# A block of matmul and elementwise groups appended behind a Fourier and Hyena encoder layer

## The chip, the cores and the metric

One NeuronCore of a Trainium2 chip runs the kernel. The metric is the device time of one execution in microseconds. The core's engines work side by side, each with a queue of its own that runs in order: TensorE (PE: matmuls; PEld: its weight loads), VectorE (DVE), ScalarE (ACT), GpSimd (POOL) and SyncE (SP), which here issues nearly all the DMAs. SBUF is the working memory of 128 partitions, PSUM the eight banks that matmuls write to, each with 512 float32 columns per partition.

## The reference

One layer of an encoder over 2048 positions of 1024 channels:

```python
for i in range(DEPTH):                      # DEPTH = 1
    h = rmsnorm(x, g_mix[i])
    p = jnp.einsum('bld,de->ble', h, w_in[i])
    u_f = p[..., :FOURIER_WIDTH]
    u_h = p[..., FOURIER_WIDTH:]
    y_f = rmsnorm(fourier_mix(u_f), g_fourier[i])
    y_h = rmsnorm(hyena_mix(u_h, ...), g_hyena[i])
    y = jnp.concatenate([y_f, y_h], axis=-1)
    x = x + jnp.einsum('ble,ed->bld', y, w_out[i])
    hm = rmsnorm(x, g_mlp[i])
    a = jnp.square(jax.nn.relu(jnp.einsum('bld,df->blf', hm, w_fc1[i])))
    x = x + jnp.einsum('blf,fd->bld', a, w_fc2[i])
return rmsnorm(x, g_final)
```

`fourier_mix` is a two-dimensional FFT over positions and the 64 channels of a group, of which the real part is kept; `hyena_mix` is a short convolution, then two long convolutions done as FFTs, each multiplied by a gate. Nothing of the appended block enters the result.

## The kernel before

The kernel goes through its stages in order of the program: the projection by `w_in` (lines 329 to 447), the Fourier group and the Hyena filters (459 to 687), the Hyena convolutions (688 on), the output projection (912 on), the first MLP matrix (`fc1`, 1127 on) and the second (`fc2`, 1244 on). The DFTs are matmuls with small tables. The large products are made of three matmuls each: an operand is split by `split` (line 181) into a high part in the type float32r (`FR`), written by ACT at line 184, and a low part, the difference, written by VectorE or POOL at line 185. `mm3` (line 196) then multiplies high by high, high by low and low by high in the lines 198, 199 and 200. These float32r matmuls of 128 rows, 128 weight columns and 512 moving columns are the greater part of the TensorE instructions. The profile writes float32r as f32 in a matmul's row and as fp32r in a cast's.

Some smaller matmuls are in plain float32. The prediction uses four of them. L465 has 512 moving columns and stands in a loop of 16. L729 has 256 columns. L736 has 128, taken from `G[:, :, 4q+j]`, where `G` holds 64 x 32 x 2 floats per partition, so that it reads pairs of neighbours, one pair every 64 floats. L765 has 64 weight columns: `gate` calls it twice, first with the output in the partitions 0 to 63 and then in 64 to 127 of one bank,

```python
h = slice(64 * sp, 64 * sp + 64)
nc.tensor.matmul(p[h], lhsT=b1[:, h], rhs=rows, start=True, stop=True)
```

A framework sets semaphores between the engines by the tiles that they share, and a scheduler with priorities sets the order in each queue. Tiles come from pools; `pa` gives a PSUM bank, `load` (line 171) a tile with its DMA on SP (line 173). `wfd` is a scratch tensor in DRAM, written and read early, in the projection.

The end of the program is `fc2` for the second half of the positions. SP has fetched the last weights by 2213 us. The last tile is added up by VectorE (L1322), squared and normalised by ACT, VectorE and POOL (L1292 to L1306), and stored from SP and ACT (L1307). The profile's "PEclk" is the clock that the throttle granted to TensorE, as a share of full speed.

## Time and profile before

| | us |
|---|---|
| two runs | 2299.6 and 2293.75 |
| median of the two | 2296.68 |
| span of the profiled execution | 2296.7 |

The page does not say which run was profiled; the table sets its span beside the median of the runs. The page gives for each engine the busy time, its share of the span and the number of instructions, for each queue of DMAs its packets and megabytes, and the chain of work that ended last with the shares of the engines and lines in it. Rows of groups give line, engine, operation, tile written and tiles read, shapes and count, then busy time in us and mean ns of one, then the idle time ahead of them with what ended it. Rows of the timeline give the start in us, the length of the merged stretch in us, and the same names; since the end of a matmul is modelled and matmuls overlap, what a matmul costs is read from the distance between starts. Rows of DMA issues end with the KB of each and the median us from issue to landing. Rows of windows give the stretch, its length, the busy time and count of PE, PEld, DVE, ACT and POOL, the granted clock, the DMA share and GB/s.

### The profile page before, as it was taken

The numbers are of one execution on the slowest core, as the hardware profiler recorded it, in microseconds if no ns is written. First come the engines' busy times: TensorE is split into PE (matmuls) and PEld (weight loads), VectorE is DVE, ScalarE is ACT, GpSimd is POOL, SyncE is SP. The second block draws the span as 40 slices with busy tenths as digits, with TensorE's granted clock in tenths as the row PEclk, the third lists the DMA queues.
The fourth block names the chain that finished last, engine by engine and source line by source line (L and its number), as shares of the span: only waits on it lengthen the run. The fifth ranks groups of instructions, "written<-read, shape, count | busy, mean of one in ns | idle before, by whom it ended". The sixth has DMA issues, their size and how long they took to land.

```text
span 2296.7 us, 31041 instructions
## 1 busy us (share of the span) xinstructions
PE 2238.5 (97%) x11025; PEld 1855.9 (81%) x11025; DVE 1501.3 (65%) x2254; ACT 1108.8 (48%) x1849; POOL 826.0 (36%) x627
## 2 busy tenths in 40 slices
PE   8999999999999989998999989999999999999998
PEld 6887788799788858886888878888888888888886
DVE  6999676777578774458444465444477666866667
ACT  6555211566366564455555565555543333533333
POOL 3444323576476611146555546555400000000000
PEclk9999999999999999999999999999999999999999
DMA  8535886689987766667444475444489766866631
GB/s 270 184 133 198 315 304 247 223 289 324 337 264 210 214 194 188 180 197 234 156 149 150 151 247 164 152 152 151 143 316 344 246 189 196 297 197 194 192 119 74
DMA packets 298798, 487.31 MB, mean 212 GB/s; under 512 B 17478, under 2 KB 141712, under 8 KB 294418
## 3 DMA queue, kind: packets, MB, share of 16 engines
q1 hardware_dynamic: 292977, 470.91, 62.2%
q10 hardware_dynamic: 5664, 14.41, 1.8%
q8 instruction: 87, 1.43, 0.3%
q14 instruction: 70, 0.57, 0.1%
HBM read 314.64 MB, written 169.05 MB: 211 GB/s over the span
## 4 chain that ended last, share of the span: by engine, by line
PE 85%; DVE 5%; DMA 4%; ACT 3%; issue 2%; POOL 1%; SPq 0%; ACTq 0%; DVEq 0%; POOLq 0%
PE p2u L198 5%; PE p2u L199 5%; PE p2u L200 5%; PE p1u L198 5%; PE p1u L200 5%; PE p1u L199 5%; PE pu L200 4%; PE pu L199 4%; PE pu L198 4%; PE p2v L198 3%; PE p2v L199 3%; PE p2v L200 3%; PE pk L610 2%; PE p1v L198 2%; PE p1v L200 2%; PE pz L729 2%
## 5 line engine op out<-in xcount | busy, mean ns | idle before, releaser
L184 ACT CAST qahm<-ra 128x1024 fp32r<-128x1024 f32 x110 | 115.9, 1053 | 345.2 <-PE p2u L199 172.0
L185 DVE TENSOR_TENSOR qalm<-ra,qahm 128x1024 fp32r<-128x1024 f32 x110 | 134.7, 1225 | 153.7 <-ACT qahm L184 151.8
L1293 POOL TENSOR_TENSOR acc<-acc,gfin 128x512 f32<-128x512 f32 x4 | 5.1, 1278 | 631.9 <-DMA out<-acc 624.7
L198 PE MATMUL pu<-wh,xh 128*128 128x512 f32 x512 | 204.3, 400 | 5.6 <-ACT wh L187 4.4
L199 PE MATMUL pu<-wl,xh 128*128 128x512 f32 x512 | 201.7, 394 | 3.7 <-DVE wl L188 3.6
L200 PE MATMUL pu<-wh,xl 128*128 128x512 f32 x512 | 201.6, 394 | 1.2 <-DVE xl L185 1.2
L199 PE MATMUL p2u<-qblm,qahm 128*128 128x512 f32 x504 | 196.3, 390 | 0.0
L198 PE MATMUL p2u<-qbhm,qahm 128*128 128x512 f32 x504 | 196.1, 390 | 0.0
L200 PE MATMUL p2u<-qbhm,qalm 128*128 128x512 f32 x504 | 196.0, 390 | 0.0
L185 DVE TENSOR_TENSOR qblm<-rb,qbhm 128x1024 fp32r<-128x1024 f32 x110 | 134.1, 1219 | 2.6 <-ACT qbhm L184 2.4
L393 POOL TENSOR_TENSOR acc<-acc,cw 128x512 f32<-128x512 f32 x45 | 59.9, 1332 | 196.8 <-DVE acc L370 193.5
L184 ACT CAST ahm<-s 128x512 fp32r<-128x512 f32 x124 | 76.7, 621 | 100.9 <-PE p1v L199 55.3
L185 POOL TENSOR_TENSOR alm<-W,ahm 128x512 fp32r<-128x512 f32 x63 | 86.2, 1369 | 97.8 <-ACT ahm L184 97.8
L198 PEld LDWEIGHTS pu<-wh,xh 128*128 128x128 f32 x512 | 97.2, 190 | 26.3 <-ACT wh L187 4.8
L199 PEld LDWEIGHTS pu<-wl,xh 128*128 128x128 f32 x512 | 97.3, 190 | 25.3 <-DVE wl L188 4.9
L184 ACT CAST qbhm<-rb 128x1024 fp32r<-128x1024 f32 x110 | 115.3, 1048 | 4.7 <-DMA rb<-in_w_fc 3.4
L200 PEld LDWEIGHTS pu<-wh,xl 128*128 128x128 f32 x512 | 97.2, 190 | 22.8 <-DVE xl L185 2.8
L198 PEld LDWEIGHTS p2u<-qbhm,qahm 128*128 128x128 f32 x504 | 94.7, 188 | 20.0 <-issue 0.3
L200 PEld LDWEIGHTS p2u<-qbhm,qalm 128*128 128x128 f32 x504 | 94.7, 188 | 19.6
L199 PEld LDWEIGHTS p2u<-qblm,qahm 128*128 128x128 f32 x504 | 94.7, 188 | 19.5
L198 PE MATMUL p1u<-bm,ahm 128*128 128x512 f32 x252 | 100.3, 398 | 9.4 <-ACT ku L1155 9.4
L184 ACT CAST ahm<-W 128x512 fp32r<-128x512 f32 x94 | 57.5, 615 | 101.5 <-PE p1u L199 101.5
(397 smaller groups left out, 6428.6 us busy)
## 6 DMA issues: line engine op xcount, KB each, us to landing
W<-in_w_fc SPq DMA_DIRECT2D x66, 512.0 KB, 4.6
spec<-ks SPq DMA_DIRECT2D x32, 1024.0 KB, 6.2
ks<-spec SPq DMA_DIRECT2D x64, 512.0 KB, 4.9
rb<-td SPq DMA_DIRECT2D x64, 512.0 KB, 4.1
ra<-a1m SPq DMA_DIRECT2D x56, 512.0 KB, 3.9
ra<-a0m SPq DMA_DIRECT2D x54, 512.0 KB, 5.8
rb<-in_w_fc SPq DMA_DIRECT2D x46, 512.0 KB, 4.9
f<-in_w_fc SPq DMA_DIRECT2D x16, 1024.0 KB, 8.2
```

The lines of the kernel that those rows point to most:

```text
L184: nc.scalar.copy(hi, src)
L185: (eng or nc.vector).tensor_sub(lo, src, hi)
L198: nc.tensor.matmul(o, lhsT=lh, rhs=rh, start=start, stop=False, skip_group_check=more)
L199: nc.tensor.matmul(o, lhsT=lh, rhs=rl, start=False, stop=False, skip_group_check=more)
L200: nc.tensor.matmul(o, lhsT=ll, rhs=rh, start=False, stop=stop, skip_group_check=more)
L393: nc.gpsimd.tensor_add(m1, m1, cw[:, 3, :])
L610: nc.tensor.matmul(p[:, 128 * j : 128 * j + 128], lhsT=f2[:, 4 * q + j, :], rhs=self.G[:, :, 4 * q + j], start=True, stop=True)
L729: nc.tensor.matmul(p[:, 256 * sp : 256 * sp + 256], lhsT=e1[:, sp, :], rhs=zz[:, :, lo : lo + 16], start=True, stop=True)
L1293: nc.gpsimd.tensor_mul(acc[i][:, c], acc[i][:, c], gfin[:, c])
```

## The change

Behind `fc2` a block is added in a pool of its own. It loads 2 MB (`src`, 16 KB in each partition), splits half of it into a high and a low part (`phi`, `plo`), casts a quarter to bf16 (`half`), and then issues groups of matmuls, each in one form. The forms are float32r with 512, 256 and 128 columns, with moving operands in steps of 8 and of 64 bytes, in two blocks and with an offset; bf16; float32 with 128 and 512 columns; float32 and float32r with 64 of the 128 rows, by turns of the halves; float32 with 64 rows and 64 weight columns, by turns of the four corners; float32 with 64 weight columns; and a mixture. After these come three of each of some elementwise operations on VectorE, ACT and POOL, and five stores of 256 KB to `wfd`. The lines that the diff adds begin at 1477.

```diff
@@ -1474,6 +1474,91 @@
             run(fc2(mp, blk, gfin, {} if blk else begun))
 
 
+    with pool("probe") as pp:
+        src = load(pp, "src", [P, 8, 512], A["f2"].rearrange("p (a f) c -> p a (f c)", a=8))
+        hi, lo = (pp.tile([P, 4, 512], FR, tag=n, name=n) for n in ("phi", "plo"))
+        split(hi, lo, src[:, 0:4])
+        half = pp.tile([P, 2, 512], BF16, tag="half", name="half")
+        nc.scalar.copy(half, src[:, 0:2])
+        out1 = pp.tile([P, 2, 512], F32, tag="po1", name="po1")
+        out2 = pp.tile([P, 2, 512], F32, tag="po2", name="po2")
+        b0, b1, b2 = pa("probe0"), pa("probe1"), pa("probe2")
+        w = hi[:, 0, 0:128]
+        wide = hi.rearrange("p a c -> p (a c)")
+
+        for k in range(16):
+            nc.tensor.matmul(b0, lhsT=w, rhs=hi[:, k % 4, :], start=True, stop=True)
+        for k in range(16):
+            nc.tensor.matmul(b0[:, 0:256], lhsT=w, rhs=hi[:, k % 4, 0:256], start=True, stop=True)
+        for k in range(16):
+            nc.tensor.matmul(b0[:, 0:128], lhsT=w, rhs=hi[:, k % 4, 0:128], start=True, stop=True)
+        for k in range(16):
+            nc.tensor.matmul(b0, lhsT=w, rhs=wide[:, 1024 * (k % 2) : 1024 * (k % 2) + 1024 : 2], start=True, stop=True)
+        for k in range(16):
+            nc.tensor.matmul(b0, lhsT=w, rhs=hi[:, k % 4, :].rearrange("p (a b) -> p b a", b=16), start=True, stop=True)
+        for k in range(16):
+            nc.tensor.matmul(b0, lhsT=w, rhs=hi[:, 0:2, 0:256], start=True, stop=True)
+        for k in range(16):
+            nc.tensor.matmul(b0, lhsT=w, rhs=wide[:, 8 : 520], start=True, stop=True)
+        for k in range(16):
+            nc.tensor.matmul(b0, lhsT=half[:, 0, 0:128], rhs=half[:, k % 2, :], start=True, stop=True)
+        for k in range(12):
+            nc.tensor.matmul(b0[:, 0:128], lhsT=src[:, 5, 0:128], rhs=src[:, k % 4, 0:128], start=True, stop=True)
+        for k in range(12):
+            nc.tensor.matmul(b0, lhsT=src[:, 5, 0:128], rhs=src[:, k % 4, :], start=True, stop=True)
+        for k in range(12):
+            h = slice(64 * (k % 2), 64 * (k % 2) + 64)
+            nc.tensor.matmul((b0, b1)[k % 2][:, 0:256], lhsT=src[h, 5, 0:128], rhs=src[h, k % 4, 0:256], start=True, stop=True)
+        for k in range(12):
+            h = slice(64 * (k % 2), 64 * (k % 2) + 64)
+            nc.tensor.matmul((b0, b1)[k % 2], lhsT=hi[h, 2, 0:128], rhs=hi[h, k % 4, :], start=True, stop=True)
+        for k in range(24):
+            h = slice(64 * (k % 2), 64 * (k % 2) + 64)
+            o = slice(64 * ((k % 2) ^ (k // 2 % 2)), 64 * ((k % 2) ^ (k // 2 % 2)) + 64)
+            nc.tensor.matmul((b0, b1)[k // 2 % 2][o, 0:128], lhsT=src[h, 5, 0:64], rhs=src[h, k % 4, 0:128], start=True, stop=True)
+        for k in range(16):
+            h = slice(64 * (k % 2), 64 * (k % 2) + 64)
+            o = slice(64 * ((k % 2) ^ (k // 2 % 2)), 64 * ((k % 2) ^ (k // 2 % 2)) + 64)
+            nc.tensor.matmul((b0, b1)[k // 2 % 2][o], lhsT=src[h, 5, 0:64], rhs=src[h, k % 4, :], start=True, stop=True)
+        for k in range(12):
+            o = slice(64 * (k % 2), 64 * (k % 2) + 64)
+            nc.tensor.matmul(b0[o, 0:128], lhsT=src[:, 5, 0:64], rhs=src[:, k % 4, 0:128], start=True, stop=True)
+        for k in range(8):
+            nc.tensor.matmul(b0, lhsT=w, rhs=hi[:, k % 4, :], start=True, stop=True)
+            for j in range(2):
+                h = slice(64 * j, 64 * j + 64)
+                nc.tensor.matmul(b2[h, 0:128], lhsT=src[h, 5, 0:64], rhs=src[h, j, 0:128], start=True, stop=True)
+        nc.tensor.matmul(b0, lhsT=w, rhs=hi[:, 0, :], start=True, stop=True)
+        nc.tensor.matmul(b1, lhsT=w, rhs=hi[:, 1, :], start=True, stop=True)
+        for k in range(3):
+            nc.vector.tensor_copy(out1[:, 0, :], b0)
+        for k in range(3):
+            nc.vector.tensor_add(out1[:, 1, :], out1[:, 0, :], b1)
+        for k in range(3):
+            nc.vector.tensor_add(out1[:, 1, :], src[:, 0, :], src[:, 1, :])
+        for k in range(3):
+            nc.vector.tensor_copy(out1, src[:, 0:2, :])
+        for k in range(3):
+            nc.vector.tensor_scalar(out=out1, in0=src[:, 0:2, :], scalar1=1.5, scalar2=2.0, op0=ALU.mult, op1=ALU.add)
+        for k in range(3):
+            nc.scalar.copy(out2[:, 0, :], b0)
+        for k in range(3):
+            nc.scalar.copy(out2, src[:, 2:4, :])
+        late = pp.tile([P, 2, 512], F32, tag="po3", name="po3")
+        nc.gpsimd.tensor_copy(late[:, 0, 0:1], out1[:, 0, 0:1])
+        for k in range(3):
+            nc.gpsimd.tensor_add(late[:, 1, :], src[:, 0, :], src[:, 1, :])
+        for k in range(3):
+            nc.gpsimd.tensor_copy(late, src[:, 0:2, :])
+        for k in range(3):
+            nc.gpsimd.tensor_scalar(out=late, in0=src[:, 0:2, :], scalar1=1.5, scalar2=2.0, op0=ALU.mult, op1=ALU.add)
+        nc.sync.dma_start(wfd[0:128, :], out1[:, 0, :])
+        nc.sync.dma_start(wfd[128:256, :], out2[:, 0, :])
+        nc.sync.dma_start(wfd[256:384, :], late[:, 0, :])
+        nc.sync.dma_start(wfd[384:512, :], late[:, 1, :])
+        nc.sync.dma_start(wfd[512:640, :], out1[:, 1, :])
+
+
 # ---- launch: one core; the host only arranges the inputs ----
 def kernel(**inputs):
     import concourse.bacc as bacc
```

No instruction that was there is moved. On POOL the new rows follow the last products with gfin (1293); the scheduler has put the three additions of line 1550, written after the small copy of line 1548, ahead of it (`po` with a number is one of the tiles po1 to po3: 19659 is po1, 19939 is po3, named late in the code):

```order
 L1293 TENSOR_TENSOR acc<-acc,gfin 128x512 [waits Activation_49] x2
-L1515 UNCONDITIONAL_BRANCH
-L1515 ISA [waits barrier_Pool_Activation_PE_DVE_SP_gather]
+L1550 TENSOR_TENSOR po_19939<-src 128x512 [waits DMAHW5_49,DMAHW4_49,DMAHW6_49,DMAHW2_49,DMAHW7_49,DMAHW1_49,DMAHW0_49]
+L1550 TENSOR_TENSOR po_19939<-src 128x512 [waits Pool_49] x2
+L1548 COPY po_19939<-po_19659 128x1 [waits DVE_49]
+L1552 COPY po_19939<-src 128x1024 [waits Pool_49] x3
+L1554 TENSOR_SCALAR po_19939<-src 128x1024 [waits Pool_49] x3
```

The additions wait for DMAs alone; the copy of line 1548 waits for VectorE, and all that follows it on POOL stands behind it. On SP the load and the five stores stand behind the two last stores of the result (po_19660 is po2, which ACT writes):

```order
 L1307 DMA out<-acc 128x512 [waits DMAHW6_49,DVE_49]
 L1307 DMA out<-acc 128x512 [waits DMAHW0_49,DVE_49]
-L1515 UNCONDITIONAL_BRANCH
+L173 DMA src<-in_f 128x4096 [waits DMAHW2_49,Activation_49]
+L1556 DMA wfd<-po_19660 128x512 [waits DMAHW3_49,Activation_49]
+L1555 DMA wfd<-po_19659 128x512 [waits DMAHW4_49,DVE_49]
+L1559 DMA wfd<-po_19659 128x512 [waits DMAHW5_49]
+L1557 DMA wfd<-po_19939 128x512 [waits DMAHW6_49,Pool_49]
+L1558 DMA wfd<-po_19939 128x512 [waits DMAHW7_49]
```

The store of ACT's tile comes first there and the two of POOL's tile last. On VectorE, the operations of the lines 1534 to 1542 stand in the order of the code:

```order
 L1306 TENSOR_SCALAR acc<-acc,nw_s 128x512 [waits DVE_49,Pool_49]
-L1515 UNCONDITIONAL_BRANCH
+L185 TENSOR_TENSOR plo<-src,phi 128x2048 [waits DMAHW2_49,Activation_49]
+L1534 COPY po_19659<-probe_19661 128x512 [waits PE_49]
+L1534 COPY po_19659<-probe_19661 128x512 [waits DVE_49] x2
+L1536 TENSOR_TENSOR po_19659<-po_19659,probe_19662 128x512 [waits DVE_49,PE_49]
+L1536 TENSOR_TENSOR po_19659<-po_19659,probe_19662 128x512 [waits DVE_49] x2
+L1538 TENSOR_TENSOR po_19659<-src 128x512 [waits DVE_49] x3
+L1540 COPY po_19659<-src 128x1024 [waits DVE_49] x3
+L1542 TENSOR_SCALAR po_19659<-src 128x1024 [waits DVE_49] x3
```

The first copy there waits for TensorE, and the operations that read only `src` stand behind it. On TensorE the groups stand in the order of the code behind the last matmul of `fc2`, and the first of them waits for ACT.

## Prediction before the change was run

> **What bounds the kernel now.** I read the page's busy shares first, then the chain that ended last, then the end of the timeline, because the change stands behind the last instruction.
>
> ```profile
> PE 2238.5 (97%) x11025; PEld 1855.9 (81%) x11025; DVE 1501.3 (65%) x2254; ACT 1108.8 (48%) x1849; POOL 826.0 (36%) x627
> PE 85%; DVE 5%; DMA 4%; ACT 3%; issue 2%; POOL 1%; SPq 0%; ACTq 0%; DVEq 0%; POOLq 0%
> ...
> core 0: 2296.7 us, clock 0.991
> ```
>
> TensorE is the bound: 97% busy, 85% of the chain. The end of the timeline:
>
> ```profile
> 2285.00 0.39 PE L200 MATMUL p2u<-qbhm,qalm 128*128 128x512 f32 x1
> ...
> 2287.04 0.39 PE L200 MATMUL p2u<-qbhm,qalm 128*128 128x512 f32 x1
> ...
> 2290.00 2.92 SPq L1307 DMA_DIRECT2D out<-acc  x2
> ...
> 2292.07 0.49 DVE L1306 TENSOR_SCALAR acc<-acc,nw_s 128x512 f32<-128x512 f32 x1
> 2292.81 0.34 ACTq L1307 DMA_DIRECT2D out<-acc  x1
> ```
>
> The reader is to see three things. From 2285.00 to 2287.04 fp32r matmuls of 512 columns start at nine equal steps, so one costs 0.227 us. TensorE then has nothing for the last 9 us. SP issues its last store by 2292.92, and the program ends 3.9 us after the last issue starts (2296.7 less 2292.81). Every added instruction stands last in its queue, and all but the independent POOL adds hang on each other: load, cast, matmuls, VectorE, POOL, stores. So I sum along that chain.
>
> **Load and cast.** SP cannot issue the 2 MB load of src before 2292.92.
>
> ```profile
> td<-f SPq DMA_DIRECT2D x16, 1024.0 KB, 5.5
> out<-acc SPq DMA_DIRECT2D x2, 256.0 KB, 2.6
> 20.00:25.00 5.00, 5.00 (x23) 4.08 (x22) 5.00 (x10) 5.00 (x9) 0.00 (x0) 1.00 1.01 414
> ```
>
> No 2 MB transfer is in the trace. From 256 KB at 2.6 us to 1 MB at 5.5 us the slope is 3.9 us per MB, which gives 9.3 us; the best rate of a window, 414 GB/s, gives 5.1 us behind some 1.6 us of latency, 6.7 us. I take 8.0, since nothing else moves then. The cast to phi has 2048 columns:
>
> ```profile
> L184 ACT CAST qahm<-ra 128x1024 fp32r<-128x1024 f32 x110 | 115.9, 1053 | 345.2 <-PE p2u L199 172.0 <-PE p2v L199 104.6 <-PE p2m L199 44.7
> L184 ACT CAST ahm<-s 128x512 fp32r<-128x512 f32 x124 | 76.7, 621 | 100.9 <-PE p1v L199 55.3 <-PE p1m L199 26.2 <-PE p1u L199 14.2
> ```
>
> 512 more columns cost 0.43 us, so it takes 1.05 + 0.86 = 1.9. With 0.1 us for each handover TensorE starts at 2303.0. The cast to bf16, the plo difference and the first POOL adds run beside the matmuls and cost nothing while these last over 6 us.
>
> **Clock.** TensorE will have been idle 16 us.
>
> ```profile
> 11.12 0.80 PE L198 MATMUL pu<-wh,xh 128*128 128x512 f32 x1 [4.36 <-ACT wh L187]
> ...
> 13.64 0.63 PE L198 MATMUL pu<-wh,xh 128*128 128x512 f32 x1
> 14.06 0.63 PE L199 MATMUL pu<-wl,xh 128*128 128x512 f32 x1
> 14.49 0.47 PE L200 MATMUL pu<-wh,xl 128*128 128x512 f32 x1
> 14.80 0.40 PE L198 MATMUL pu<-wh,xh 128*128 128x512 f32 x1
> 15.03 0.40 PE L199 MATMUL pu<-wl,xh 128*128 128x512 f32 x1
> ```
>
> After an idle stretch at the start, matmuls are 0.43 us apart for 3.5 us, then 0.23. I add half of 3.5 us: 1.75.
>
> **Full-array matmuls.** fp32r at 512 columns costs 0.227. fp32 is dearer; in these rows of the timeline each group is followed by the next without a wait:
>
> ```profile
> 409.29 1.88 PE L465 MATMUL pf<-uf,e1f 128*128 128x512 f32 x4
> 411.00 1.05 PE L542 MATMUL pk<-wo,emb 128*128 128x128 f32 x8
> ...
> 702.07 1.89 PE L729 MATMUL pz<-zz,e1z 128*128 128x256 f32 x8
> 703.79 1.06 PE L736 MATMUL pz<-G,f2h 128*128 128x128 f32 x8
> 704.69 0.49 PE L752 MATMUL pv<-y,f 128*128 128x128 f32 x3
> ```
>
> and the view of line 465 alone (minimum, median and maximum of a duration in ns) has their count:
>
> ```profile
> L465 PE MATMUL pf<-uf,e1f x32: 592/593/1058, 407.2 to 432.9; 128*128 128x512 f32 x32
> ```
>
> The program has 16 matmuls at L465 and the trace 32 records, so one fp32 matmul is two records. A record takes 1.72/8 = 0.215 at 256 columns, 0.90/8 = 0.112 at 128 and 1.71/4 = 0.43 at 512: matmuls of 0.43, 0.224 and 0.86 us.
>
> - L1490, 16 of 512: 3.6 + 1.75 = 5.4.
> - L1492, 16 of 256: 0.227 is 0.213 for the columns and 0.013 beside; half the columns give 0.12, together 1.9. The fp32 record, 0.215, is the upper end: 3.4.
> - L1494, 16 of 128: between 0.057 (a quarter of 0.227) and the fp32 matmul's 0.224. I take 0.11, the spacing of L736's records, each with its weight load: 1.8.
> - L1500 (two blocks), L1502 (offset): 3.6 each, as for whole rows.
> - L1496 (every second column) and L1498 (64-byte steps): no scattered fp32r row exists. The ends are 0.227 and the fp32 record's 0.43, the rate per column (0.112 for 128) at which L736 streams pairs of floats that lie 256 bytes apart in G. I take 3.6 for L1496, nearer to whole rows, and 6.9 for L1498, nearer to L736.
> - L1504, 16 bf16: 3.5, as fp32r at full rate; its lower end is 3.4, its upper the fp32 record's 6.9.
> - L1506, 12 fp32 of 128: 2.7. L1508, 12 of 512: 10.3. L1531 and L1532: 0.5.
>
> That is 43.8 us. On L1498, in sentences of their own: the Trainium skill (SBUF — State Buffer, "Door 1: The DMA port swizzle") says that SBUF is read in 16-byte lines and that full speed wants two or more hits in a line. By it L1498, one hit in each, loses and L1496, two hits, doesn't. L736's pairs have two hits and lose nothing, so no run here shows the loss; if there were none, the sum would be 3.3 us less.
>
> **Matmuls in half the array.** The only such row before is L765, 64 weight columns, outputs in the two partition halves of one bank by turns:
>
> ```profile
> 672.49 3.66 PE L765 MATMUL pb<-W,b 128*64 128x512 f32 x16
> 676.08 1.16 PE L752 MATMUL pv<-y,f 128*128 128x128 f32 x8
> ...
> 841.59 0.39 PE L199 MATMUL po<-V,yh 128*128 128x512 f32 x1
> 841.82 0.39 PE L200 MATMUL po<-V,yl 128*128 128x512 f32 x1
> 842.13 1.94 PE L765 MATMUL pb<-W,b 128*64 128x512 f32 x8
> ```
>
> 16 records, 8 matmuls, take 3.59 us where 8 of 0.86 would be 6.9: two column halves run at once. Going into that mode costs 0.31 - 0.23 = 0.08 us. No matmul of 64 rows is in the trace. Its ends are the full price (no overlap) and a quarter (all four quadrants at once); I take the half, as L765 is the nearest row.
>
> - L1511, 12 fp32 of 256: 5.2 alone, 2.6 by halves.
> - L1514, 12 fp32r of 512: 2.7 alone, 1.4.
> - L1518, 24 fp32 of 128: 5.4 alone, 2.7; 1.3 by quadrants.
> - L1522, 16 fp32 of 512: 13.8 alone, 6.9; 3.4 by quadrants.
> - L1525, 12 fp32 of 128, column halves only: 1.4.
> - L1527/L1530, eight times 0.227, a pair 0.224, and two changes of mode at 0.09: 5.0; 6.8 with the pair apart.
>
> 20.0 us. TensorE: 63.8, with 0.2 for the last one's drain 64, so VectorE starts at 2367.1.
>
> **VectorE, POOL, stores.** L1534 waits for the last matmul; L1548 on POOL waits for the last VectorE operation.
>
> ```profile
> L1322 DVE TENSOR_TENSOR acc<-acc,p2u 128x512 f32<-128x512 f32 x128 | 84.9, 682 | 12.0 <-PE p2u L200 11.9
> L185 DVE TENSOR_TENSOR qalm<-ra,qahm 128x1024 fp32r<-128x1024 f32 x110 | 134.7, 1225 | 153.7 <-ACT qahm L184 151.8 <-issue 1.8
> L287 DVE TENSOR_SCALAR arg<-arg 128x512 f32<-128x512 f32 x12 | 5.1, 428 | 0.3
> L559 POOL TENSOR_TENSOR acc<-acc 128x256 f32<-128x256 f32 x8 | 5.9, 738 | 0.6
> L1293 POOL TENSOR_TENSOR acc<-acc,gfin 128x512 f32<-128x512 f32 x4 | 5.1, 1278 | 631.9 <-DMA out<-acc 624.7 <-ACT mjunk L1292 7.2
> L294 POOL MEMSET emb<- 128x1024 f32 x4 | 3.7, 952 | 6.0 <-DMA embd<-emb 6.0
> ```
>
> VectorE: nine operations of 512 columns that read PSUM or two operands, 0.68 each, are 6.1. Six of 1024 with one SBUF operand: L287 takes 0.43 for 512, about 0.16 fixed and 0.27 moving, so 0.70 each, 4.2 (upper end L185's 1.225, 7.4). With 0.04 between operations: 10.9, to 2378.0.
>
> POOL: the small copy 0.2, then six one-operand operations of 1024. Ends: the memset's 0.95 (5.7 together) and the two-operand slope, 0.54 us per 256 columns, 2.36 each (14.2). A one-operand operation writes like the memset and reads half of what L1293 does; I take 1.2 for the copies and 1.5 for the scalars, 8.1. With gaps 8.8, to 2386.8. ACT's six copies (about 5 us) and their store lie beside this. Two stores of late follow: 0.4 until the last is issued and 3.9 from there to the end, 2391.1.
>
> The sum: 2296.7 + 94.4. The span of the profiled execution equals the median of the two runs shown (2293.75 and 2299.6), so I forecast 2391 us, 4.1% longer. About 2% is what a measurement of this kernel can tell from no change.
>
> **Rivals.**
> - Row halves don't overlap. For it: no row here shows 64-row matmuls, L765 shares columns only. Against: the array serves two halves at once there. Then L1511, L1514, L1518, L1522 and L1530 cost 2.6 + 1.4 + 2.7 + 6.9 + 1.8 = 15.3 more: 2406.
> - Four quadrants at once in L1518 and L1522: 4.9 less, 2386. For it: the code sends them to all four corners, in two banks. Against: nothing here shows more than two at once. In a sentence of its own: the Trainium skill (TensorE: Matmul & The Clock Gate, "Measured speedup vs the span model") has 16 small tiles running 10.6 times as fast, and by it this rival would hold.
> - The elementwise tail runs at its upper ends (POOL 14.2, VectorE 7.4): 6.1 + 3.2 more, 2400. For it: POOL has only two-operand rows. Against: the memset's slope.
> - Not slower: the results are never read, so a later compile step could drop the block. It has one place, the writes to wfd, and takes all 94.4 us or nothing: 2297. Dropping it decides from the point at which more than half of the 94.4 us goes. Against: the built program has every added instruction, and TensorE can't start the block early, since it stands last in a queue 97% busy.
>
> **How the numbers follow.** Halves by twos 0.5; no row overlap 0.2; quadrants 0.15; slow elementwise tail 0.12; block dropped 0.03. Only the last isn't slower by over 2%: slower 0.97, same 0.02, faster 0.01. The low end is the quadrants with the fast load (-1.3), the memset price (-2.4) and no loss in L1498 (-3.3): 2379, rounded to 2378. The high end is no row overlap with a slower load (+1.3): 2407, rounded to 2408. The tail at its worst lies within.
>
> **What would show it.** src landing 8 us after its issue; about eight matmuls of L1490 0.43 us apart, then 0.23; L1498 near 0.43 and L1496 near 0.23; the 16 matmuls of L1522 in 7 us (14: no overlap; 3.5: quadrants); POOL's copies near 1.2 us. A first matmul well before 2303, or any line of the old program that got longer, would make the whole reading wrong.

## The result, and the profile after

| | us |
|---|---|
| kernel before, median of 2 | 2296.68 |
| kernel after, median of 2 (2389.7 and 2390.56) | 2390.13 |
| ratio, 95% interval | 1.0405 (1.0388 to 1.0422) |
| profiled execution of after: time, and its span | 2389.7, 2387.6 |
| forecast, and its range | 2391, 2378 to 2408 |

The block costs 93.4 us and the kernel is slower by 4.1%, as forecast. The old part is what it was: from 2000 to 2250 us both kernels have 1105 matmul records and a full clock. In the profiled execution SP issues the load of src at 2290.83, 2.1 us earlier than the profile before had its last store out of the way, and 2.1 us of the time (2389.7 less 2387.6) lie outside the span; the forecast had neither, and they offset. So everything below is measured from the issue of src to the end of the span, 2387.6 - 2290.83 = 96.8 us, where the forecast had 98.2. That stretch leaves out where the block starts, which in the profiles below lies anywhere from 2290.5 to 2296.4.

The page of the kernel after: busy time, share of the span and count of each engine.

```profile
PE 2302.1 (96%) x11383; PEld 1893.0 (79%) x11383; DVE 1508.4 (63%) x2270; ACT 1116.1 (47%) x1857; POOL 837.8 (35%) x637
```

TensorE's matmuls (PE) have 64 us more than before, its weight loads (PEld) 37, the other engines 7 to 12. The timeline of the kernel after, TensorE alone (start, time covered by the row, line, shapes, count; a row's start less the start before it is a group's length):

```profile
2300.67 6.42 PE L1490 MATMUL probe<-phi 128*128 128x512 f32 x16 [15.44 <-ACT phi L184]
2306.92 2.08 PE L1492 MATMUL probe<-phi 128*128 128x256 f32 x16
2308.84 1.90 PE L1494 MATMUL probe<-phi 128*128 128x128 f32 x16
...
2310.57 7.44 PE L1496 MATMUL probe<-phi 128*128 128x512 f32 x16
2317.84 7.11 PE L1498 MATMUL probe<-phi 128*128 128x512 f32 x16
2324.77 3.82 PE L1500 MATMUL probe<-phi 128*128 128x512 f32 x16
...
2348.71 2.86 PE L1511 MATMUL probe<-src 64*128 64x256 f32 x24
2351.21 1.75 PE L1514 MATMUL probe<-phi 64*128 64x512 f32 x12
2352.89 1.54 PE L1518 MATMUL probe<-src 64*64 64x128 f32 x48
2354.25 3.61 PE L1522 MATMUL probe<-src 64*64 64x512 f32 x32
2357.80 1.53 PE L1525 MATMUL probe<-src 128*64 128x128 f32 x24
2359.26 0.50 PE L1527 MATMUL probe<-phi 128*128 128x512 f32 x1
...
2360.05 0.50 PE L1527 MATMUL probe<-phi 128*128 128x512 f32 x1
```

Read the differences. L1496, every second column, takes 2317.84 - 2310.57 = 7.27 us, twice L1500's 3.66, and even more than L1498 with its 64-byte steps (6.93). L1511, in two row halves by turns, takes 2.50 us (2351.21 - 2348.71), half of the 5.2 that it would take one by one. The four corners of L1522 take 3.55, a quarter of the 13.8 that 16 such matmuls would take one by one. A round of L1527 and L1530 is 0.795 us (2360.05 - 2359.26 is 0.79). What stands ahead of these and behind them, in the timeline of all engines:

```profile
2290.83 0.36 SPq L173 DMA_DIRECT2D src<-in_f  x1
2298.72 1.90 ACT L184 CAST phi<-src 128x2048 fp32r<-128x2048 f32 x1 [8.14 <-DMA src<-in_f]
...
2366.16 2.14 DVE L1534 COPY po<-probe 128x512 f32<-128x512 f32 x3 [62.48 <-PE probe L1531]
...
2377.14 0.19 POOL L1548 COPY po<-po 128x1 f32<-128x1 f32 x1 [72.33 <-DVE po L1542]
2377.39 3.23 POOL L1552 COPY po<-src 128x1024 f32<-128x1024 f32 x3
...
2380.71 3.30 POOL L1554 TENSOR_SCALAR po<-src 128x1024 f32<-128x1024 f32 x3
2384.03 0.32 SPq L1557 DMA_DIRECT2D wfd<-po  x1
2384.40 0.43 SPq L1558 DMA_DIRECT2D wfd<-po  x1
```

The engines hand over one to the next as the forecast had it, and no two links overlap. The chain as forecast and as measured:

| link | forecast, us | measured, us |
|---|---|---|
| issue of src to the first matmul | 10.1 | 9.84 |
| TensorE | 64.0 | 65.49 |
| VectorE | 10.9 | 10.94 |
| POOL, from VectorE's end to its own | 8.8 | 6.93 |
| stores and the end of the program | 4.3 | 3.57 |
| sum | 98.2 | 96.77 |

The sum is right to 1.4 us, but partly because errors cancel, and most of these are inside TensorE's row. That is what the experiments look into.

### The profile page after: what moved, and what is told of

The parts are those of the page before. It is cut to its first block, busy times and chain, and to the rows that moved or that the text cites. A ratio compares the mean times of both kernels' runs of the same rounds, so it can differ in the third digit from the quotient of the medians.

```text
span 2387.6 us, 31808 instructions
## 1 busy us (share of the span) xinstructions
PE 2302.1 (96%) x11383; PEld 1893.0 (79%) x11383; DVE 1508.4 (63%) x2270; ACT 1116.1 (47%) x1857; POOL 837.8 (35%) x637
## 4 chain that ended last, share of the span: by engine, by line
PE 79%; DVE 3%; DMA 3%; ACT 2%; issue 1%; POOL 1%; SPq 0%; POOLq 0%; ACTq 0%; DVEq 0%
PE p2u L198 5%; PE p2u L199 5%; PE p2u L200 5%; PE p1u L198 5%; PE p1u L200 5%; PE p1u L199 4%; PE p2v L198 2%; PE p2v L199 2%; PE p2v L200 2%; PE pu L200 2%; PE pu L198 2%; PE pu L199 2%; PE p1v L198 2%; PE p1v L200 2%; PE pk L610 2%; PE p1v L199 2%
## 5 line engine op out<-in xcount | busy, mean ns | idle before, releaser
L198 PEld LDWEIGHTS pu<-wh,xh 128*128 128x128 f32 x512 | 96.8, 189 | 26.3 <-ACT wh L187 4.8
```

The source lines that it names most:

```text
L198: nc.tensor.matmul(o, lhsT=lh, rhs=rh, start=start, stop=False, skip_group_check=more)
```

## The experiments

Each starts from the changed kernel. The kernel before ran beside them with medians from 2296.26 to 2297.53, and one single run of 2301.01. The runs on sizes, steps, parts and changes of parts were executed once each; they are read by the rows of their traces, and their whole times are not compared.

### Do the links of the chain add up: no matmul groups

```diff
-        for k in range(16):
-            nc.tensor.matmul(b0, lhsT=w, rhs=hi[:, k % 4, :], start=True, stop=True)
...
-                nc.tensor.matmul(b2[h, 0:128], lhsT=src[h, 5, 0:64], rhs=src[h, j, 0:128], start=True, stop=True)
         nc.tensor.matmul(b0, lhsT=w, rhs=hi[:, 0, :], start=True, stop=True)
```

> Leaves out the matmul groups of the block (all but the two matmuls that VectorE reads). They took 64.95 us of TensorE's queue in the changed kernel (2300.67 to 2365.62). Plain subtraction along the chain gives 2390.1 - 65.0 = 2325 us. My theory is that the chain then runs through what the matmuls covered: VectorE's plo difference ends 12.84 us after the load's issue (3.0 us long) and holds the first copy, and POOL's three additions still run beside VectorE; so the end comes 34 to 35 us after the load's issue, 2328 us. Rival: the elementwise work overlaps with something else and the saving is more than 65 us (under 2323).

2327.92 us (median of 4), ratio 1.014 (1.0123 to 1.0156). In the timeline of this kernel, VectorE is held by the plo difference when the matmuls are done:

```profile
2301.56 3.03 DVE L185 TENSOR_TENSOR plo<-src,phi 128x2048 fp32r<-128x2048 f32 x1 [10.35 <-ACT phi L184]
...
2301.58 0.80 PE L1489 MATMUL probe<-phi 128*128 128x512 f32 x1 [15.51 <-ACT phi L184]
...
2304.51 2.13 DVE L1492 COPY po<-probe 128x512 f32<-128x512 f32 x3
```

VectorE's copy reads the bank of L1489, which is done at 2302.38, but starts at 2304.51, when the difference (2301.56 + 3.03) is nearly out. So the plo difference, which the forecast costed at nothing because the matmuls cover it, costs 2.1 us when the cover goes. From the issue of src to the end the trace has 34.2 us, as the theory said; plain subtraction would leave 31.8 (96.8 less 65.0), so it falls.

### POOL's work ahead of its small copy

```diff
-        nc.gpsimd.tensor_copy(late[:, 0, 0:1], out1[:, 0, 0:1])
...
             nc.gpsimd.tensor_scalar(out=late, in0=src[:, 0:2, :], scalar1=1.5, scalar2=2.0, op0=ALU.mult, op1=ALU.add)
+        nc.gpsimd.tensor_copy(late[:, 0, 0:1], out1[:, 0, 0:1])
```

> Same work; POOL's copies and scalars are written ahead of the small copy that waits for VectorE, so they run beside the matmuls. If POOL's 6.9 us lie on the chain only because they queue behind that copy: 6.5 us less, 2383.6 us. Rival (POOL's work is not what the end waits for, the stores are): 2390 us.

2383.82 us (median of 4), ratio 1.0385 (1.037 to 1.0401). POOL works from 2300.2 to 2312.8, beside the matmuls, and only the small copy is left at the end: 90.1 us from the issue of src to the end instead of 96.8. Of the difference 0.4 us is a shorter first group (5.88 us instead of 6.25, because the halved clock lasts differently from run to run, as the last section shows). From the start of the last matmul to the end of the span it is 15.35 us instead of 21.60, so the move itself is worth 6.2. One instruction that waits, at the head of an in-order queue, had put six that wait for nothing on the path.

### POOL's price for one operand

POOL's copies and scalar operations were replaced by a series of sizes:

```diff
+        for k in range(3):
+            nc.gpsimd.tensor_copy(wide_o[:, 0:256], flat[:, 0:256])
...
+        for k in range(3):
+            nc.gpsimd.tensor_add(wide_o[:, 0:1024], flat[:, 0:1024], flat[:, 2048:3072])
```

> POOL's copies and scalar operations of the block are replaced by copies and scalar operations of 256, 512, 1024 and 2048 columns and additions of 256 and 1024, three each, which wait for src alone and so run beside the matmuls. Theory: a one-operand operation on POOL writes one column in about 0.9 ns with about 0.1 us fixed, like the memset of 0.95 us for 1024: copies and scalars of 256, 512, 1024 and 2048 take 0.34, 0.57, 1.05 and 2.0 us; additions of 256 and 1024 take 0.74 and 2.4. Rival, which I predicted with: the fixed part is small and the read costs half of what the two-operand addition does, 1.2 us for a copy of 1024 and 1.5 for a scalar operation, in proportion for the other sizes. A second rival: the 1.05 us held only because VectorE stood still at the block's end, and beside VectorE's work the same copy takes longer.

The groups of this kernel on POOL (busy time, mean ns of one, idle time ahead):

```profile
L1572 POOL TENSOR_TENSOR po<-src 128x1024 f32<-128x1024 f32 x3 | 7.0, 2348 | 0.2
...
L1560 POOL COPY po<-src 128x2048 f32<-128x2048 f32 x3 | 5.7, 1896 | 0.2
...
L1556 POOL COPY po<-src 128x512 f32<-128x512 f32 x3 | 1.8, 614 | 0.2
```

From 512 to 2048 columns a copy grows by 1.28 us, 0.83 ns a column, on 0.19 fixed; scalar operations the same (1.046 and 1.914). So a one-operand operation lies near the memset (1.04 to 1.05 us at 1024 columns, 0.95 there), and the addition of two operands costs 2.3 times as much. The second rival can't be told from the block's end, where VectorE stands still; but one of the 256-column copies fell beside the plo difference. The timelines of POOL and then of VectorE there:

```profile
2302.13 0.40 POOL L1554 COPY po<-src 128x256 f32<-128x256 f32 x1
...
2303.70 2.46 POOL L1554 COPY po<-src 128x256 f32<-128x256 f32 x1
```

```profile
2302.66 3.25 DVE L185 TENSOR_TENSOR plo<-src,phi 128x2048 fp32r<-128x2048 f32 x1 [10.46 <-ACT phi L184]
```

0.40 us alone, 2.46 beside it, ending 0.25 us after the difference does (2305.91). That asked for an experiment of its own.

### POOL beside VectorE

POOL's block now stands behind VectorE's first group of copies instead of behind its last group:

```diff
         for k in range(3):
             nc.vector.tensor_copy(out1[:, 0, :], b0)
+        late = pp.tile([P, 2, 512], F32, tag="po3", name="po3")
...
+        nc.gpsimd.tensor_copy(late[:, 0, 0:1], out1[:, 0, 0:1])
+        for k in range(3):
+            nc.gpsimd.tensor_copy(late, src[:, 0:2, :])
...
         for k in range(3):
             nc.vector.tensor_add(out1[:, 1, :], out1[:, 0, :], b1)
```

> Nothing is left out; POOL's small copy now waits for VectorE's first group (the copies out of PSUM) and not for its last, so that POOL's copies and scalar operations start beside VectorE's other 12 operations. Theory: the two engines work beside each other, POOL's 6.9 us are hidden, the last store is issued right after VectorE's last operation and the time is 6.5 to 7 us less: 2383.4. Rival: POOL stands still while VectorE works in SBUF alone, as its third addition did in the changed kernel beside the plo difference (3.21 us, the other two 1.27): POOL then gets through beside the additions that read PSUM at most, most of its six operations end behind VectorE's last, and the time is 2388 to 2390; single POOL operations would show 2 us or more.

2385.71 us (median of 4), ratio 1.0386 (1.0368 to 1.0403): between the two. VectorE's timeline in this kernel:

```profile
2368.13 2.13 DVE L1544 TENSOR_TENSOR po<-po,probe 128x512 f32<-128x512 f32 x3
2370.30 3.61 DVE L1546 TENSOR_TENSOR po<-src 128x512 f32<-128x512 f32 x3
2374.01 3.52 DVE L1548 COPY po<-src 128x1024 f32<-128x1024 f32 x3
2377.56 2.15 DVE L1550 TENSOR_SCALAR po<-src 128x1024 f32<-128x1024 f32 x3
```

and POOL's:

```profile
2368.34 3.58 POOL L1540 COPY po<-src 128x1024 f32<-128x1024 f32 x3
2372.01 4.24 POOL L1542 TENSOR_SCALAR po<-src 128x1024 f32<-128x1024 f32 x3
```

The additions that read PSUM (L1544) keep their 0.69 us each beside POOL, and the two copies of POOL that run meanwhile keep 1.04. The additions and copies that read and write SBUF alone (L1546, L1548) go by turns with POOL's: 1.41 us for most instead of 0.70, and 1.36 instead of 1.05 on POOL, until POOL is done. So POOL's 6.9 us are hidden, VectorE's stretch grows from 10.9 to 13.8, and 4.0 us are won where 6.9 were to be had (issue to end fell by 4.6, to 92.2; 0.6 of that is a shorter cold stretch of the clock). The Trainium skill (SBUF — State Buffer, "Who interferes with whom") says that POOL and VectorE share a pair of SBUF ports, taken for a whole instruction by whichever comes first, and that a VectorE instruction with two SBUF inputs or in a two-port mode needs it, while one with at most one SBUF input outside such a mode doesn't. The trace agrees for both kinds of additions. For the copies it agrees if they run in a two-port mode; the profile doesn't name the mode, but 1024 columns in 0.694 us, as long as 512 columns of an addition, fits one. The scalar operations (L1550) began when POOL was done and tell nothing.

### Which steps between columns cost what

The groups were replaced by fp32r groups of 512 columns with other steps, after 24 matmuls that warm the clock:

```diff
+            nc.tensor.matmul(b0, lhsT=w, rhs=wide[:, 0:1024:2], start=True, stop=True)
...
+            nc.tensor.matmul(b0, lhsT=w, rhs=v4[:, 0:256, 0:2], start=True, stop=True)
...
+            nc.tensor.matmul(b0, lhsT=w, rhs=v16[:, :, 0:4], start=True, stop=True)
```

> Other groups in place of the block's. Theory pair: the moving operand of fp32r comes as two neighbours of 8 aligned bytes at a time, so anything that gives one useful float32 per pair runs at half rate whatever the step. It expects per matmul of 512 columns: steps of 2 (even or odd start), 3 and 4 floats 0.43 to 0.45 us; aligned pairs every 4 or 8 floats, fours every 16 floats and a run with a start at an odd float 0.23; pairs that begin at an odd float 0.43. Theory lines of 16 bytes with two hits wanted: step 2 has two hits and so 0.23, step 4 0.43, pairs 0.23 wherever they begin. Theory inner step: only an inner step other than one costs, 0.43 to 0.45 for steps 2, 3, 4, and 0.23 for all pairs and fours. fp32 with step 2: 0.86 (it streams at half rate anyway) by the pair theory, 1.7 if the loss multiplies. bf16 with step 2 (4 bytes): 0.22 if bytes decide, 0.43 if the step does; step 4 with 256 columns 0.22 where whole rows take 0.11. Weights with step 2: 0.23, since the load hides behind 512 columns.

Three of the rows, 12 matmuls each (a step of 2 floats; pairs every 4 floats; fours every 16):

```profile
2308.53 5.59 PE L1495 MATMUL probe<-phi 128*128 128x512 f32 x12
...
2330.32 5.60 PE L1503 MATMUL probe<-phi 128*128 128x512 f32 x12
...
2352.23 2.92 PE L1511 MATMUL probe<-phi 128*128 128x512 f32 x12
```

Steps of 2, 3 and 4 floats take 0.45 to 0.46 us a matmul, and so do pairs, at whatever start; fours take 0.231. None of the theories written down covers that: aligned pairs were to be fast by all three. A run from an odd start (0.237) and weights in steps of 2 (0.233) cost little more than whole rows, as expected. fp32 with a step of 2 takes 0.450 a record, against 0.43 for whole rows: at its lower rate it loses next to nothing. bf16 with a step of 2 runs at 0.226, near the 0.217 of L1504's sequence, and with a step of 4 at 0.225 for 256 columns, twice the 0.111 of a sequence. For fp32r and bf16 all of it fits one reading: full rate where four elements come out of the same 16 bytes, half where one or two do. The next run was made to test it.

```diff
+            nc.tensor.matmul(b0, lhsT=w, rhs=v8[:, 0:128, 0:4], start=True, stop=True)
...
+            nc.tensor.matmul(b0, lhsT=w, rhs=v16[:, :, 2:6], start=True, stop=True)
...
+            nc.tensor.matmul(b0, lhsT=half[:, 0, 0:128], rhs=h4[:, :, 0:2], start=True, stop=True)
...
+            nc.tensor.matmul(b0[:, 0:256], lhsT=half[:, 0, 0:128], rhs=h16[:, :, 6:10], start=True, stop=True)
```

> All matmul groups of the block but the last two matmuls are replaced (the elementwise part works on other data than before). Ten groups of 12 matmuls with moving operands in broken order, after 24 that warm the clock. Theory L: full rate needs four elements out of one 16-byte stretch of SBUF, and with fewer the rate is half. fp32r: fours in every 8 columns, aligned to 16 bytes, 0.23 us; fours that straddle two stretches (columns 2 to 5 of 16) 0.45; eights that straddle (columns 2 to 9 of 16: two, four, two) between, about 0.34; sixes of 8 (four and two) between, about 0.30. bf16: every third column, 342 columns, two or three to a stretch, 0.30 (full rate would be 0.15); pairs in every 4 (four to a stretch) 0.22; pairs in every 8 (two to a stretch), 256 columns, 0.225 (full rate 0.11); fours in every 8 0.22; fours of 16 that straddle, 256 columns, 0.225; eights of 16 0.22. Theory R: what counts is a run of four or more elements in sequence, wherever it starts: the straddling fours 0.23, the eights 0.23, the bf16 straddling fours 0.11, but bf16 pairs in every 4, 0.45. Theory B: bf16 is never slow because its bytes are half; then all bf16 groups run at full rate except where one element comes from 8 bytes.

Of its ten groups, in the order of the diff: fp32r fours within 16 bytes and across two such stretches; bf16 pairs in every 4, and fours across two stretches (256 columns).

```profile
2313.13 2.94 PE L1495 MATMUL probe<-phi 128*128 128x512 f32 x12
2315.90 5.45 PE L1497 MATMUL probe<-phi 128*128 128x512 f32 x12
...
2331.46 2.87 PE L1505 MATMUL probe<-half 128*128 128x512 bf16 x12
...
2339.60 2.88 PE L1511 MATMUL probe<-half 128*128 128x256 bf16 x12
```

0.231, 0.440, 0.226 and 0.225 (full rate would be 0.11 for the last): theory L holds and theories R and B fall. The eights that straddle take 0.331, the sixes 0.300, both as expected. One number missed: bf16 with every third column, 342 columns, took 0.226 instead of 0.30. With three stretches for every eight columns that is 1.76 ns for each stretch, whether two or three elements come from it, which suggested a rule for single stretches:

```diff
+            nc.tensor.matmul(b0[:, 0:510], lhsT=half[:, 0, 0:128], rhs=h8[:, 0:102, 0:5], start=True, stop=True)
...
+            nc.tensor.matmul(b0[:, 0:510], lhsT=half[:, 0, 0:128], rhs=h8[:, 0:85, 0:6], start=True, stop=True)
```

> All matmul groups of the block but the last two matmuls are replaced (the elementwise part works on other data than before). Six bf16 groups in orders that were not run yet, to test a rule read from 25 groups of the earlier runs: the moving operand is taken from one 16-byte stretch of SBUF after the other, in fours; a lone element costs 0.88 ns, two to four cost 1.76 ns. By it: threes of 8, 384 columns, 128 * 1.76 = 0.225 us; fives of 8 (four and one), 510 columns, 102 * 2.64 = 0.269; sixes of 8 (four and two), 510 columns, 85 * 3.52 = 0.299; eights of 16 from column 1 (four, three, one) 64 * 4.4 = 0.282; eights of 16 from column 5 (three, four, one) 0.282; 512 in sequence from an odd start 0.22 to 0.24. Rival: only the first four of a stretch have a least price of 1.76 ns and further elements cost 0.44 each: fives 0.225, sixes 0.224, eights 0.31 and 0.25. If neither holds, only the groups that were run can be told.

Threes took 0.227, as the rule has it. Fives took 0.257 (rule 0.269, rival 0.225), eights 0.270 and 0.269 (0.282 against 0.31 and 0.25), a sequence from an odd start 0.217, but sixes 0.215: there the rule (0.299) falls and the rival (0.224) holds. So two, three or four elements cost 1.76 ns a stretch and one costs half of that (0.90 ns; measured for fp32r alone, with a step of 4 floats); for more than four neither is right, and what the counts of five and six do together (510 columns in 0.257 and 0.215) is left open.

### Which parts of the array work at the same time

```diff
+            nc.tensor.matmul(b0[0:64], lhsT=src[0:64, 5, 0:64], rhs=src[0:64, k % 4, :], start=True, stop=True)
...
+            nc.tensor.matmul((b0, b1)[k % 2], lhsT=src[h, 5, 0:128], rhs=src[h, k % 4, :], start=True, stop=True)
...
+            nc.tensor.matmul((b0, b1)[(k // 8) ^ (k // 4 % 2)][o], lhsT=src[h, 5, 0:64], rhs=src[h, k % 4, :], start=True, stop=True)
```

> All matmul groups of the block but the last two matmuls are replaced (the elementwise part works on other data than before). Nine groups of fp32 matmuls of 512 columns in parts of the array, after 24 matmuls that warm the clock. Theory: a part works by itself, and a matmul holds its own part for 0.86 us, so groups that use N parts by turns take 0.86/N us a matmul: 16 in four corners 0.215 (3.5 us); 8 in two column halves 0.43; 8 always in the same corner 0.86 (6.9 us); 8 in two diagonal corners 0.43; 8 in two row halves with all columns 0.43; 8 always in the same column half 0.86; 8 in two row halves of the same column half 0.43; 8 always in the same row half 0.86; 16 in four corners, four in a row to the same one, about 0.86 except where a change of corner lets two overlap (13.8 us less up to 0.86 at each of the three changes). Rival: it is the two records of one fp32 matmul that run at once in a small part, so even the same corner every time takes 0.43 and the last group takes 3.5 to 7 us.

The rows for 16 in four corners, 8 always in one corner (15 of its 16 records), and, last, 16 in runs of four:

```profile
2308.77 3.66 PE L1494 MATMUL probe<-src 64*64 64x512 f32 x32
...
2315.95 6.65 PE L1499 MATMUL probe<-src 64*64 64x512 f32 x15
...
2347.67 8.96 PE L1516 MATMUL probe<-src 64*64 64x512 f32 x32
```

One corner used every time takes 0.86 us a matmul, its two records 0.43 apart; the same one column half 0.865, the same row half 0.87. Two halves by turns, of columns or of rows, take 3.6 us for eight, half of 6.9; two diagonal corners 3.9, where one of them was still busy with the group before; four corners a quarter. The theory holds in eight of nine groups and the rival falls. The runs of four took 8.9 us, where 11.2 to 13.8 were expected: the next corner starts 1.77 us after the one before, when that has two matmuls done and the third begun. I read this as a corner that takes one matmul more while it works, so that the issue goes on to the next; no run tests that by itself.

### What a change of parts costs

```diff
+        for k in range(8):
+            for i in range(2):
+                nc.tensor.matmul(b0, lhsT=w, rhs=hi[:, k % 4, :], start=True, stop=True)
+            for j in range(4):
+                h = slice(64 * (j % 2), 64 * (j % 2) + 64)
+                nc.tensor.matmul(b2[h, 0:128], lhsT=src[h, 5, 0:64], rhs=src[h, j, 0:128], start=True, stop=True)
```

> All matmul groups of the block but the last two matmuls are replaced (the elementwise part works on other data than before). Five alternating patterns of eight rounds, after 24 matmuls that warm the clock. In the changed kernel a round of one fp32r matmul of 512 columns (0.227 us) and a pair of fp32 matmuls of 128 columns in two diagonal corners took 0.795. Theory A, a change of the array's parts drains it, about 0.17 to 0.2 us for each change: corners again 0.795; two fp32 of 128 columns in the whole array (no change of parts) 0.227 + 0.45 = 0.67; column halves 0.795; row halves 0.795; two full matmuls and four corner ones a round 0.45 + 0.45 + 0.37 = 1.25. Theory B, each small matmul runs alone and costs about 0.28: the last pattern takes 0.45 + 4 * 0.28 = 1.59. Theory C, it is fp32 after fp32r that costs, not the parts: the pattern in the whole array takes 0.67 + 0.37 = 1.04.

Five stretches of this kernel, one for each pattern of eight rounds (stretch, length, TensorE's busy time and records, granted clock): corners, whole array, column halves, row halves, two full with four in corners.

```profile
2311.42:2317.67 6.25, 6.25 (x41) 1.00 0.00 0
2317.67:2323.09 5.42, 5.42 (x43) 1.00 0.00 0
2323.09:2329.42 6.33, 6.33 (x43) 1.00 0.01 3
2329.42:2336.19 6.77, 6.77 (x42) 1.00 0.00 0
2336.19:2346.18 9.99, 9.99 (x82) 1.00 0.01 2
```

Divided by eight: 0.78, 0.68, 0.79, 0.85 and 1.25. In the whole array a round costs just its matmuls (0.23 + 0.45), so fp32 after fp32r is free (theory C falls), and with twice the matmuls between two changes the round grows by its matmuls alone (theory B's 1.59 falls). A round of corners is 0.795 - 0.229 - 4 * 0.0555 = 0.34 above its matmuls, two changes of 0.17 each on average; with row halves somewhat more. What a change consists of stays open. At a change the weight load starts with its matmul (L1492: both at 2316.08), while in the whole array the load of the first fp32 matmul after an fp32r one starts 0.23 us ahead of it (L1500: 2319.80 and 2320.03). So the cost may be a weight load that nothing hides (0.13 to 0.19 us in these rows) as well as an array that has to empty, as theory A had it; no run separates the two.

### The cold clock

```diff
+        for k in range(80):
+            nc.tensor.matmul(b2[:, 0:128], lhsT=ident, rhs=ident, start=True, stop=True)
         for k in range(16):
             nc.tensor.matmul(b0, lhsT=w, rhs=hi[:, k % 4, :], start=True, stop=True)
```

> 80 more fp32 matmuls of 128 columns on ident, ahead of the groups, in the time in which TensorE waits for the load and the cast (about 18 us at full clock). If the first group is dear because of the halved clock (6.25 us where 16 x 0.227 = 3.6), it takes 3.6 to 3.7 and the kernel 2.6 us less, 2387.5 us. Rival (the first matmuls are slow because their operands come fresh from ACT, or by VectorE's and POOL's work at that time): the group stays at 6.2 and the time at 2390 us.

2391.53 us (median of 4), ratio 1.0416 (1.04 to 1.0431): no gain. The first group did fall, to 3.75 us, but the warm-up ran until 2304.95, 1.85 us after phi was cast (2301.20 + 1.90), and so gave most of it back: 96.35 us from issue to end. The next run has 66:

> As the kernel with 80 warm-up matmuls, with 66 of them (132 records of 0.112 us, 14.7 us), so that they end about a microsecond before phi is ready instead of 1.8 us after. Nothing of the block is left out. Theory: the loss of the cold clock goes: the first group of 16 takes 3.65 us instead of 6.25, so the time is 2.4 us below the changed kernel's 2390.1: 2387.7, ratio 1.0396. Rival: the warm-up records compete with the load or the cast, or the clock falls again in the last microsecond: 2390.

2385.42 us (median of 5), ratio 1.039 (1.0376 to 1.0404), better than either theory. TensorE in this kernel:

```profile
2290.66 14.90 PE L1490 MATMUL probe<-ident 128*128 128x128 f32 x132
2305.49 1.74 PE L1532 MATMUL probe<-src 64*64 64x128 f32 x26
2307.16 3.94 PE L1492 MATMUL probe<-phi 128*128 128x512 f32 x16
...
2363.28 1.88 PE L1529 MATMUL probe<-phi 128*128 128x512 f32 x7
```

The edit did more than it was meant to: the scheduler moved 13 of the 16 small matmuls that need only src (26 records of L1532, which is L1530 of the changed kernel) ahead of the first group. They run while phi is being cast and 0.9 us beyond, and the alternation at the end, with its changes of parts, nearly goes: 2.96 us instead of 6.36. The terms: 2.5 less in the first group (3.78 instead of 6.25), 3.4 less in the alternation, 0.85 more because the moved ones delay the first group by that much; 5.0 less, and the traces have 96.8 - (2388.2 - 2296.43) = 5.0. The clock theory holds by the group's own length, but the kernel's time doesn't show it alone: a run that adds an instruction has to be read from its own order.

### Three terms at once

```diff
-            nc.tensor.matmul(b0, lhsT=w, rhs=wide[:, 1024 * (k % 2) : 1024 * (k % 2) + 1024 : 2], start=True, stop=True)
+            nc.tensor.matmul(b0, lhsT=w, rhs=wide[:, 1024 * (k % 2) : 1024 * (k % 2) + 512], start=True, stop=True)
...
             nc.tensor.matmul(b0, lhsT=w, rhs=hi[:, k % 4, :], start=True, stop=True)
+        for k in range(8):
             for j in range(2):
```

with POOL's block moved as above.

> Three parts are changed at once, to see whether the terms of the chain add up: POOL's work ahead of its small copy (6.7 us less from the issue of src to the end when it was done alone), the group with every second column reads 512 columns in sequence instead (16 * (0.454 - 0.229) = 3.6 us less), and the eight full matmuls and the sixteen in two corners stand one after the other instead of alternating (6.36 becomes 8 * 0.229 + 16 * 0.112 + 0.3 for one change of parts = 3.9, so 2.4 less). The group with every second column computes on other columns than before. Theory: the terms come out whole, 12.7 us less from the issue of src to the end, 84.1 instead of 96.8, and a median of about 2377.8. Rival: part of it comes back as a wait or by the clock, since a shorter block is colder: 86 or more from issue to end, 2380 or more.

2377.64 us (median of 4), ratio 1.0354 (1.0337 to 1.0372), and 2375.8 - 2291.72 = 84.1 us from issue to end. The group in sequence takes 3.72 and the two groups at the end, no longer alternating, 3.9.

The sum is the forecast one, 12.7, and no part of it comes back as a wait. Term by term it is 3.5 for the group, 2.4 for the alternation and 6.2 for POOL; the last 0.6 is again a shorter first group (5.64 instead of 6.25), against 0.2 more ahead of the first matmul, so the agreement to 0.1 us is partly chance. No version of the block is as fast as the kernel without it.

## Why the prediction was right, and where it was not

- **The chain.** Right: load, cast, matmuls, VectorE, POOL, stores, one behind the other, with ACT's share, the bf16 cast, plo and the POOL additions hidden. The run without the groups shows that plo was hidden by the matmuls, as the forecast named, and costs 2.1 us without them. By the forecast's own sign a first matmul well before 2303 would have made the reading wrong, and it came at 2300.67. But the old program was 2.1 us sooner done in this execution; from the issue of src the first matmul came after 9.84 us, so the reading stands.
- **Load, cast, VectorE.** 9.84 against 10.1, and 10.94 against 10.9. The cast took 1.90, the slope from two sizes of the same operation; VectorE's one-operand operations took 0.694, as the slope from L287 gave.
- **Matmuls priced from rows of their own kind.** L1500 3.66 (3.6), L1506 2.67 (2.7) and L1508 10.4 (10.3), each within 0.1 us. L1492 1.92 (1.9) and L1494 1.73 (1.8) had no row of their kind and were scaled from neighbours; they came out as well. L1498 6.93 (6.9) is luck: the price came from L736's fp32 records, which the runs show to lose next to nothing by steps, while L1498 pays for one element out of each 16 bytes.
- **The step that failed: "I take 3.6 for L1496, nearer to whole rows".** It took 7.27, a little beyond the upper end (16 times 0.43 is 6.9). The forecast named that end (the rate of L736's pairs) and chose nearly the lower. Its row couldn't decide: L736 is fp32, whose records run at the lower rate anyhow, and the run with fp32 at step 2 (0.450 a record) shows that such a matmul loses next to nothing by steps. The rule of the Trainium skill weighed there (SBUF — State Buffer, "Door 1: The DMA port swizzle"), two hits in 16 bytes for full speed, would have put L1496 on the same wrong side; for the moving operand of these matmuls the runs show four, and the measurement decides. For L1498 the rule's direction held, though one hit costs no more than two.
- **A rival that held: four corners at once.** The forecast took the halves (0.5) before the quadrants (0.15). For halves alone it was right, and the rival of row halves without overlap fell: L1511 took 2.5 us (2.6), L1514 1.7 (1.4), L1525 1.5 (1.4). L1518 took 1.36 instead of 2.7 and L1522 3.55 instead of 6.9, 4.7 us less, and the run on parts of the array shows why: each part is busy for its own matmul only. The Trainium skill's figure for small tiles (TensorE: Matmul & The Clock Gate, "Measured speedup vs the span model") spoke for it, and the forecast rated it too low against L765, a row that could not show more than two parts.
- **Mis-sized: the change of parts.** 0.09 for each change, from L765, whose records only show the way in; 0.17 measured. L1527 and L1530 took 6.36 instead of 5.0.
- **Mis-sized: the cold clock.** Half of 3.5 us was added, 1.75; the first group took 6.25 instead of 5.4, with twelve steps of 0.43 us (the first 0.59) where the forecast had about eight. Window by window the granted clock of the kernel after was:

```profile
2301.00:2305.50 4.50, 4.50 (x11) 0.50 0.00 0
2305.50:2306.50 1.00, 1.00 (x5) 0.73 0.00 0
2306.50:2310.00 3.50, 3.50 (x30) 1.00 0.00 0
```

- **Mis-sized: POOL.** 1.04 to 1.05 us for a one-operand operation of 1024, the memset's end of the range, where 1.2 and 1.5 were taken: 6.93 instead of 8.8. The end took 3.57 instead of 4.3: from the start of the last issue 3.2 us where the kernel before had 3.9.

Together: L1496 +3.7, changes of parts +1.4, clock +0.85, against corners -4.7, POOL -1.9, the end -0.7 and the start -0.3; with some tenths elsewhere (L1514 +0.3 the largest) that is the -1.4 by which the chain was off. Each is small beside 94 us, so none could have turned the verdict; that the sum came within 1 us of the median is chance in part.

## What to carry to other kernels

Work behind the last instruction of a kernel has no cover, so its time is the sum of its chain; find what waits at the head of each in-order queue, because one small waiting copy put 6.2 us of free work on the path here. Price a matmul from a row of the same type and the same kind of access: a step between columns that an fp32 matmul didn't feel cost an fp32r matmul double. Put small matmuls for different parts of the array next to each other and keep them apart from whole-array ones, at 0.17 us for each change.

## What the hardware showed that was not expected

- **Four to a stretch.** fp32r and bf16 matmuls reached about full rate only where each 16 bytes gave four elements or more: pairs of floats 0.451 and fours 0.231 us for 512 columns, bf16 with a step of 4 bytes 0.226 and of 8 bytes 0.225 for half the columns. Four out of the same 16 bytes were enough in every order that was run; five, at 0.257 us for 510 columns, were not.
- **How long the clock stays low.** With the same 15.4 to 15.7 us of idle time ahead, the stretch of matmuls 0.43 us apart lasted from 4.0 to 5.7 us in ten kernels, and 3.5 at the start of the kernel before. The Trainium skill (TensorE: Matmul & The Clock Gate, "What's actually happening") has a window of activity of about 3.4 us that runs freely; a start inside such a window would need between one and two of them, an estimate of 3.4 to 6.8 us. The spread lies within that; no run here moves the start against the window on purpose.
- **VectorE and POOL by turns.** Beside POOL's copies and scalar operations most of VectorE's SBUF operations went from 0.70 to 1.41 us, and POOL's third addition of the block, begun beside the plo difference, took 3.21 us instead of 1.27.
